# Front pairs of a two-layer hybrid encoder: products P2 and P4 summed in PSUM, the second pair on sums that stay on chip, norms turned later

## The chip, the cores and the metric

One core of one Trainium2 chip runs the whole program in one launch. The metric is the time of an execution on the device in microseconds (us). An engine works through its own instruction list in order; engines wait for each other through semaphores. The names are those of the profile: PE is TensorE (matmuls), PEld its weight loads, DVE VectorE, ACT ScalarE, POOL GpSimd, SP SyncE, which here only issues transfers.

## The reference

All 512 tokens go through two layers of the same form, 2048 features wide.

```python
def hybrid_layer(x, w_in, w_out, g_pre, g_post, w_alpha, b_alpha, g_gla, g_att, rel_bias):
    h = rmsnorm(x, g_pre)
    z = h @ w_in
    gq, gk, gv, gg, ga, aq, ak, av, ag = split_columns(z)
    log_a = jax.nn.log_sigmoid((ga @ w_alpha + b_alpha).astype(jnp.float32)) / GLA_TAU
    o_gla = gla_chunk_causal(gq, gk, gv, log_a)          # reshapes to heads left out
    o_gla = rmsnorm(o_gla, g_gla) * jax.nn.silu(gg)
    o_att = chunk_band_attention(aq, ak, av, rel_bias)
    o_att = rmsnorm(o_att, g_att) * jax.nn.silu(ag)
    y = jnp.concatenate([o_gla, o_att], axis=-1) @ w_out
    return x + rmsnorm(y, g_post)
```

The change concerns the columns `ag` and `gg` of the input projection (the two gates, each two blocks of 512 columns) and the silu behind them.

## The kernel before, in words

**Products.** A pair of 512-column blocks of the input projection is computed with seven products in place of eight, by a fast scheme for 2 x 2 blocks. The activations are cut into two token halves and two feature halves (A11, A12, A21, A22), the weights into blocks of the pair. P1 and P2 use A11 and A12, P4 uses A22, and P5, P6, P3, P7 use the sums S1, S2, S4, S3 of these blocks. Each product has four contraction chunks `c` of 256 rows. Operands are kept as a high and a low part, so one chunk is 12 matmuls of 128 x 512: two halves of the chunk, two token tiles `t`, three combinations (high x high, high x low, low x high). "A product" below is one such chunk.

**What a product needs.** `Job.load` fetches its weight tile on SP's queue (512 KB; `raw`, or `H` for the tile that lives through a pair). `Job.high` casts it to its high part `wh` on ACT, after DVE has added `raw` to `H` (P5, P6, P4) or subtracted (P7). `Job.low` makes the low part `wl` on DVE. Four buffers each of `raw`, `H`, `wh` and `sa`, three of `wl`, and `ahead()` keep this some three to five products ahead of TensorE.

**Results.** A `Pair` accumulates in PSUM in two banks X, two banks Y and, for early pairs, two banks Z. `copies` keeps a result in SBUF (`ev`) by ACT; `combine` adds a kept copy to a finished bank by DVE into a temporary `t`, and `gate_consume` puts the silu (ACT, L781) on it and stores it by POOL.

**Front.** Each layer starts with two early pairs, `FRONT` = (AG0, AG1), (GG0, GG1). First come P1 and P2 of pair 0 and of pair 1 (the head), then P5, the middle (P6 and P3 mixed), P7 and P4 of pair 0, and the same of pair 1. Then the AV pair and the rest of the layer follow. Beside the products run tasks, advanced by `pump`, so many steps per product (`rate`): `token_sums` makes the 16 sums (DVE L683; split by ACT L109 and DVE L110; stored to DRAM by POOL), from `full` tiles such as `g8` and `g11`. Pair 0 (`direct`) takes the sums from SBUF and reads only A22 back (`sa<-A`); pair 1 reads all 16 sums (`sa<-S`) and A22 again, 512 KB each, on SP's queue.

**Norms.** `token_norms` squares the token rows (ACT L506), takes the power -1/2 on POOL (L493), turns the result with a TensorE transpose (L586) and stores the row. In layer 0, `first_norms(1)` and `load_forget_gate(0)` (which loads w_alpha and casts it, L763) stand in the task list ahead of the head. The order in which tasks and products issue instructions in the program is the order on each engine.

Of the kernel before, what the change touches and what calls it, by code (L numbers as in the profile page):

```python
# [35 lines left out]
def hybrid_trunk(  # L36
# [113 lines left out]
    PROD_END = early_head(C_END) + early_rest(C_END)  # L150
    LEFT = {"P5": "S1", "P6": "S2", "P3": "S4", "P7": "S3", "P4": "A22"}
# [6 lines left out]
    class Job:  # L158
# [8 lines left out]
        def load(self):  # L167
# [29 lines left out]
            src = (so_d if end else sa_d)[self.l].get((LEFT.get(k), c))  # L197
# [38 lines left out]
    for l in range(L):  # L236
        infos = [{"early": True, "direct": True}, {"early": True, "second": True}]
        for (b0, b1), pr in zip(FRONT, infos):
            stream += [Job(l, k, c, b0, b1, pr) for k, c in early_head(C_IN)]
# [130 lines left out]
    class Pair:  # L370
        def __init__(self, l, pair, consume, feature_major=False, early=False, end=False, scaled=True, direct=False,
                     y_banks=pair_banks):
            self.l, self.b0, self.consume = l, pair[0], consume
            self.feature_major, self.early, self.end = feature_major, early, end
            self.scaled, self.direct = scaled, direct
            self.banks = {"X": pair_banks, "Y": y_banks, "Z": aux_banks}
            self.target = {"P1": "X", "P5": "Y", "P6": "X", "P3": "Y", "P7": "X", "P2": "Y", "P4": "X"}
            self.starts = ["P1", "P5", "P2"]
            if early:
                self.target.update(P2="Z", P4="Y")  # L380
                self.starts.append("P4")
# [3 lines left out]
        def copies(self, name, src):  # L385
            self.keep[name] = []
            for t in range(2):
# [5 lines left out]
                self.keep[name].append(e)  # L393

# [11 lines left out]
        def finished(self, k, t):  # L406
# [12 lines left out]
        def operand(self, job, k, c):  # L419
            if job.a is not None:  # L420
                return job.a
            if k in ("P1", "P2", "P4"):
# [6 lines left out]
        def matmuls(self, job, k, c):  # L429
# [5 lines left out]
            for kk in range(2):  # L435
                if self.feature_major:
# [11 lines left out]
                else:  # L448
                    for t in range(2):
                        tok = slice(kk * 256 + t * P, kk * 256 + (t + 1) * P)  # L450
                        ops = ((0, job.wh), (0, job.wl), (1, job.wh))
                        for m, (part, rhs) in enumerate(ops):
                            nc.tensor.matmul(  # L453
                                out_ps[t], a[:, part, tok], rhs[:, kk, :],
                                start=(fresh and kk == 0 and m == 0),
                                stop=(c == self.last and kk == 1 and m == 2), skip_group_check=True,
                            )
            spent.add((self.l, LEFT.get(k), c))

        def run(self, prods, rate=0.0, skip=0, after=None):  # L460
            pace = Pace(rate, skip)
            for k, c in prods:
# [3 lines left out]
                if c == self.last:  # L466
# [48 lines left out]
    def load_row(half, j, src, q):  # L515
# [3 lines left out]
        elif j == 0:  # L519
            row = [slot(tag, [1024]) for tag in XS1]  # L520
# [29 lines left out]
    def load_first(i):  # L550
# [7 lines left out]
        if i in (5, 7, 12, 14):  # L558
            half, j = divmod((5, 7, 12, 14).index(i), 2)
            with tc.issue_after(last_load[0]):  # L560
                rows[half, j] = load_row(half, j, x, nc.sync)
# [13 lines left out]
    def token_norms(l, half, xs):  # L575
# [9 lines left out]
        ps = aux()  # L585
        nc.tensor.transpose(ps[0:2, 0:P], r, ident)  # L586
        row = t2((P,))
        nc.vector.tensor_copy(row[0:2], ps[0:2, 0:P])
        nc.gpsimd.dma_start(r_d[l][half], row[0:2])
        normed.add((l, half))  # L590
        yield
# [123 lines left out]
    def token_sums(l):  # L715
        order = products(C_IN, "S1") + [({"P6": "S2", "P3": "S4"}[k], c) for k, c in middle(C_IN)]
        order += products(C_IN, "S3")
        return make_sums(
            l, False, STAGE,
            lambda c: (full[0, c][:, 0, :], full[0, c][:, 1, :], full[1, c][:, 0, :], full[1, c][:, 1, :]), order=order,  # L720
# [50 lines left out]
    tasks.append(first_norms(1))  # L771
    tasks.append(load_forget_gate(0))

    def layer(l):
# [102 lines left out]
        if l:  # L877
# [3 lines left out]
            Pair(l, FRONT[0], gate_consume(1), early=True, scaled=False, direct=True, y_banks=aux_banks),  # L881
            Pair(l, FRONT[1], gate_consume(0), early=True, scaled=False),
# [6 lines left out]
        front[1].run(early_rest(C_IN), rate=0.25)  # L889
        drain()  # L890
# [571 lines left out]
```

## Time and profile before

| | |
|---|---|
| median of 3 runs (lowest to highest) | 1642.57 us (1642.13 to 1644.08) |
| profiled execution | 1638.18 us, span 1636.4 us |
| granted TensorE clock, mean | 0.995 |
| busy: PE, PEld, DVE, ACT, POOL | 98%, 83%, 78%, 56%, 10% |
| read from and written to DRAM | 412.93 MB, 71.06 MB; 296 GB/s over the span |
| front of layer 0, of layer 1 (about) | 5 to 198 us, 820 to 1009 us |

PE's busy share counts each matmul up to a modelled end, so that neighbours overlap; where PE is slowed a little, its busy share hardly shows it. The number of matmuls in a stretch does.

### The profile page before, as it was taken

Reading aid. Unit: us, or ns where it says so; the run is one execution under the profiler, and the core shown is the slowest. Engines: PE = TensorE matmul, PEld = TensorE weight load, DVE = VectorE, ACT = ScalarE, POOL = GpSimd, SP = SyncE. Lnnn points to the kernel's source line nnn. Section 1 sums busy time; section 2 is a strip of 40 time slices with the busy share of each in tenths; the row PEclk is TensorE's granted clock in tenths of the full one; section 3 lists DMA queues with packets and bytes.
Section 4 is the critical chain, followed back from the end, with each engine's and each line's share of the span. In section 5 each row is a group of like instructions: output and inputs, shape, how many; then the busy total and the mean of one; then the engine's idle time right before and its main releaser. Section 6 shows DMA issues by size and latency. Waiting matters only on the chain.

```text
span 1636.4 us, 24588 instructions
## 1 busy us (share of the span) xinstructions
PE 1598.3 (98%) x8818; PEld 1354.3 (83%) x8818; DVE 1270.3 (78%) x1626; ACT 918.3 (56%) x1520; POOL 165.8 (10%) x258
## 2 busy tenths in 40 slices
PE   9899999999999999999998999999999999999997
PEld 5577789999988887788786877899999888777886
DVE  7797777786877876778779977777868778766887
ACT  8554544466676545555685545444566765345553
POOL 1120000000101101310122100000011011023100
PEclk9999999999999999999999999999999999999999
DMA  9899987867868698898868998868588686979986
GB/s 370 343 347 372 375 291 249 295 221 248 294 225 292 224 328 307 297 375 313 329 234 303 356 361 342 318 223 314 179 294 291 218 290 216 353 260 349 368 303 235
DMA packets 155419, 486.73 MB, mean 297 GB/s; under 512 B 16956, under 2 KB 36036, under 8 KB 155296
## 3 DMA queue, kind: packets, MB, share of 16 engines
q1 hardware_dynamic: 132704, 406.83, 70.3%
q0 software_dynamic: 22016, 77.37, 12.3%
q8 instruction: 70, 1.15, 0.3%
q10 hardware_dynamic: 576, 0.95, 0.2%
q14 instruction: 53, 0.43, 0.1%
HBM read 412.93 MB, written 71.06 MB: 296 GB/s over the span
## 4 chain that ended last, share of the span: by engine, by line
PE 88%; DMA 5%; DVE 3%; ACT 2%; issue 1%; SPq 0%; DVEq 0%; POOL 0%; POOLq 0%; ACTq 0%
PE mm L453 44%; PE mm L443 20%; PE mm L347 10%; PE ax L453 6%; PE ax L974 2%; DMA raw<-in_w_dram 2%; DMA H<-in_w_dram 2%; DVE wl L227 1%; PE ax L957 1%; PE ax L1140 1%; DMA sa<-A 1%; PE ax L1174 1%; DVE H L211 1%; PE ax L936 1%; PE ax L937 1%
## 5 line engine op out<-in xcount | busy, mean ns | idle before, releaser
L453 PE MATMUL mm<-wh,sa 128*128 128x512 f32 x1536 | 486.3, 392 | 4.5 <-DMA sa<-A 2.1
L222 ACT CAST wh<-H 128x1024 fp32r<-128x1024 f32 x247 | 259.0, 1052 | 244.7 <-PE mm L453 92.7
L222 ACT CAST wh<-raw 128x1024 fp32r<-128x1024 f32 x248 | 261.2, 1053 | 233.7 <-PE mm L453 99.8
L227 DVE TENSOR_TENSOR wl<-H,wh 128x1024 fp32r<-128x1024 f32 (+1 forms) x249 | 302.6, 1218 | 107.0 <-PE mm L453 40.3
L227 DVE TENSOR_TENSOR wl<-raw,wh 128x1024 fp32r<-128x1024 f32 x248 | 303.0, 1223 | 105.2 <-PE mm L453 31.2
L453 PEld LDWEIGHTS mm<-wh,sa 128*128 128x128 f32 x1536 | 287.3, 188 | 68.6 <-issue 3.1
L453 PE MATMUL mm<-wl,sa 128*128 128x512 f32 x768 | 299.8, 390 | 0.0
L443 PE MATMUL mm<-sa,wh 128*128 128x256 f32 x1280 | 237.4, 286 | 0.0
L443 PEld LDWEIGHTS mm<-sa,wh 128*128 128x128 f32 x1280 | 199.8, 191 | 0.3
L453 PE MATMUL mm<-wh,a 128*128 128x512 f32 x576 | 189.4, 397 | 5.1 <-ACT wh L222 3.5
L211 DVE TENSOR_TENSOR H<-H,raw 128x1024 f32<-128x1024 f32 x152 | 184.6, 1220 | 10.3 <-DMA raw<-in_w_dram 6.6
L443 PE MATMUL mm<-sa,wl 128*128 128x256 f32 x640 | 180.6, 283 | 0.0
L453 PEld LDWEIGHTS mm<-wl,sa 128*128 128x128 f32 x768 | 144.2, 188 | 29.4
L453 PEld LDWEIGHTS mm<-wh,a 128*128 128x128 f32 x576 | 106.9, 188 | 34.3 <-ACT wh L222 5.7
L493 POOL TENSOR_TENSOR sm<-sm,mhalf 128x4 f32<-128x4 f32 (+2 forms) x40 | 56.5, 1412 | 756.4 <-DVE sm L990 520.4
L443 PEld LDWEIGHTS mm<-sa,wl 128*128 128x128 f32 x640 | 122.3, 191 | 0.1
L453 PE MATMUL mm<-wl,a 128*128 128x512 f32 x288 | 112.6, 393 | 1.6 <-DVE wl L227 1.6
L443 PE MATMUL mm<-a,wh 128*128 128x256 f32 x512 | 94.9, 285 | 0.0
L347 PE MATMUL mm<-wh,a 128*128 128x512 f32 x256 | 82.8, 393 | 0.0
L443 PEld LDWEIGHTS mm<-a,wh 128*128 128x128 f32 x512 | 80.3, 191 | 0.2
L214 DVE TENSOR_TENSOR raw<-H,raw 128x1024 f32<-128x1024 f32 x64 | 78.2, 1221 | 2.1 <-DMA raw<-in_w_dram 1.6
L443 PE MATMUL mm<-a,wl 128*128 128x256 f32 x256 | 72.4, 283 | 0.0
(206 smaller groups left out, 2358.9 us busy)
## 6 DMA issues: line engine op xcount, KB each, us to landing
raw<-in_w_dram SPq DMA_DIRECT2D x336, 512.0 KB, 5.6
sa<-S SPq DMA_DIRECT2D x192, 512.0 KB, 4.7
H<-in_w_dram SPq DMA_DIRECT2D x63, 512.0 KB, 5.0
sa<-A SPq DMA_DIRECT2D x56, 512.0 KB, 7.4
S<-g POOLq DMA_DIRECT2D x32, 512.0 KB, 4.7
oS<-g POOLq DMA_DIRECT2D x32, 512.0 KB, 6.3
sa<-oS SPq DMA_DIRECT2D x32, 512.0 KB, 5.1
sg<-t POOLq DMA_DIRECT2D x32, 256.0 KB, 5.9
```

Of the source, the lines that this page charges most:

```text
L211: nc.vector.tensor_tensor(out=h, in0=h, in1=r, op=ALU.add)
L214: nc.vector.tensor_tensor(out=r, in0=h, in1=r, op=ALU.subtract)
L222: last_cast[0] = nc.scalar.copy(self.wh, src).ins
L227: last_low[0] = nc.vector.tensor_tensor(out=self.wl[:, kk, :], in0=self.src[:, kk, :], in1=self.wh[:, kk, :].bitcast(F32), op=ALU.subtract ...
L347: mm = nc.tensor.matmul(pss[o], a[:, part, t], rhs[:, kk, :], start=(i == 0 and kk == 0 and m == 0), stop=(i == n - 1 and kk == 1 and m == 2),
L443: nc.tensor.matmul(dst, lhs[:, kk, f], a[:, part, tok], start=(fresh and kk == 0 and m == 0 and ft % 2 == 0), stop=(c == self.last and kk ...
L453: nc.tensor.matmul(out_ps[t], a[:, part, tok], rhs[:, kk, :], start=(fresh and kk == 0 and m == 0), stop=(c == self.last and kk == 1 and m ...
L493: return nc.gpsimd.tensor_tensor(out=out_r, in0=v, in1=mhalf[:, : v.shape[-1]], op=ALU.pow).ins
L936: nc.tensor.matmul(ps[:, :n], self.qh[:, t], self.kl[:, :n], start=False, stop=False)
L937: nc.tensor.matmul(ps[:, :n], self.ql[:, t], self.kh[:, :n], start=False, stop=True)
L957: nc.tensor.transpose(ps[:, j * P : (j + 1) * P], self.prob[i][:, j * P : (j + 1) * P], ident)
L974: nc.tensor.matmul(o, self.pt[i][:, j * P : (j + 1) * P], av[hd // 4, j // 2][:, j % 2, (hd % 4) * P : (hd % 4 + 1) * P], start=(j == 0), ...
```

## The change: seeded PSUM, resident sums, a new head order, later norms

- The head's order becomes P1 of pair 0, P1 of pair 1, P2 of pair 0, P2 of pair 1, at 2.7 task steps per product in place of 2.0.
- A front pair is `seeded`. P2 accumulates into P1's banks X, and the silu reads PSUM directly, without DVE's combine. For P6, `open` takes new banks X and Y, and ACT copies P1's kept result into X. After P7, ACT copies X into Y, and P4 accumulates on Y. The banks Z and the copies of x after P7 are not used any more.
- Pair 1 uses the last eight sums (`SUMS[8:]`) from SBUF, and A22 is loaded once, for both pairs, into slots of `full` tiles (g8, g14, g11, g15).
- The norm's transpose and the store of its row are delayed by eight task steps (`turn`). In layer 0, `first_norms(1)` and `load_forget_gate(0)` go to the front of the task list after the head; the token rows for the second half are loaded at jobs 15 and 17 of the stream (12 and 14 before), into g12 and g13.

```diff
+    SUMS = products(C_IN, "S1") + [({"P6": "S2", "P3": "S4"}[k], c) for k, c in middle(C_IN)] + products(C_IN, "S3")
+    RESIDENT = SUMS[8:] + products(C_IN, "A22")
...
-            if src is not None and (k == "P4" or not (p and p.get("direct"))):
-                until(lambda: (self.l, end, LEFT[k], c) in made)
+            if src is None or p.get("direct") and k != "P4" or p.get("second") and (name, c) in RESIDENT:
+                return
+            until(lambda: (self.l, end, name, c) in made)
+            if p.get("direct"):
+                until(lambda: (self.l, end, "S3", c // 2) in made)
+                self.a = S_on[self.l, name, c] = slot(("g8", "g14", "g11", "g15")[c], [2, 512], F32R)
+            else:
                 self.a = rtile("sa", (2, 512), F32R)
-                nc.sync.dma_start(flat(self.a), src)
+            nc.sync.dma_start(flat(self.a), src)
...
+            if seeded:
+                self.target.update(P2="X", P4="Y")
+                self.starts.remove("P2")
...
+        def open(self, *names):
+            for name in names:
+                self.acc[name] = self.banks[name]()
+            for t in range(2):
+                nc.scalar.copy(self.acc["X"][t], self.keep["p1"][t])
...
+            elif self.seeded:
+                self.consume(0, {"P2": 0, "P4": 1}[k], t, out, None)
...
+                order = [(kk, t) for kk in range(2) for t in range(2)]
+                if self.seeded and (k, c) in (("P7", self.last), ("P4", self.first)):
+                    order.sort(key=lambda z: z[1])
...
+                        if k == "P7" and self.seeded:
+                            for t in range(2):
+                                nc.scalar.copy(self.acc["Y"][t], self.acc["X"][t])
                         for t in range(2):
                             self.finished(k, t)
-                        if k == "P7" and self.early:
+                        if k == "P7" and self.early and not self.seeded:
                             self.copies("x", self.acc["X"])
...
-        if i in (5, 7, 12, 14):
-            half, j = divmod((5, 7, 12, 14).index(i), 2)
+        if i in (5, 7, 15, 17):
+            half, j = divmod((5, 7, 15, 17).index(i), 2)
...
+        def turn():
+            ps = aux()
+            nc.tensor.transpose(ps[0:2, 0:P], r, ident)
...
         normed.add((l, half))
+        delayed.append([8, turn])
...
     tasks.append(prep_first())
-    tasks.append(first_norms(1))
-    tasks.append(load_forget_gate(0))
...
-        for pair in front:
-            pair.run(early_head(C_IN), rate=2.0)
+        for k in ("P1", "P2"):
+            for pair in front:
+                pair.run(products(C_IN, k), rate=2.7)
+        if l == 0:
+            tasks[0:0] = [first_norms(1), load_forget_gate(0)]
+        front[0].open("Y", "X")
         front[0].run(early_rest(C_IN), rate=1.0)
         drain()
         tasks.append(forget_gate())
+        front[1].open("X", "Y")
         front[1].run(early_rest(C_IN), rate=0.25)
```

Three places in the order of instructions. First TensorE in layer 0, before, where P2 of pair 1 starts: `mm_561` and `mm_562` are the banks of pair 1's P1, `ax_704` one of its banks for P2, `a_37` the operand A12, `norm` the norm.

```order
L453 MATMUL mm_561<-wl_575,a_36_329 128x512
L453 MATMUL mm_562<-wh_527,a_36_329 128x512
L453 MATMUL mm_562<-wl_575,a_36_329 128x512
L586 MATMUL ax_671<-cst,norm_208 2x128
L453 MATMUL ax_704<-wh_577,a_37_334 128x512
L453 MATMUL ax_704<-wl_609,a_37_334 128x512
L453 MATMUL ax_705<-wh_577,a_37_334 128x512
```

TensorE after the change, where P5's third chunk starts (`mm_787`, `mm_788` are pair 0's Y banks, `g_89` and `g_93` the sums S1 of the second and third chunk):

```order
L475 MATMUL mm_788<-wl_755,g_89_599 128x512
L475 MATMUL mm_788<-wh_739,g_89_599 128x512
L613 MATMUL ax_1051<-cst,norm_208 2x128
L475 MATMUL mm_787<-wh_758,g_93_622 128x512
L475 MATMUL mm_788<-wh_758,g_93_622 128x512
```

The transpose of the second norm has moved from ahead of P2 of pair 1 to the middle of P5, eight products later.

ScalarE in layer 0 around the start of P5, before. `t_139` is the combined P2 of a pair, `wh_721` and the next two are P5's first casts, the squares of the token rows (L506) stand earlier, among P2's casts:

```order
L506 ACTIVATE t_109_647,sm_639<-sg_618 128x512
L222 CAST wh_694<-raw_666 128x1024
L222 CAST wh_721<-H_211 128x1024
L109 CAST g_127_726<-g_48_388 128x512
L222 CAST wh_745<-H_217 128x1024
L109 CAST g_131_750<-g_61_428 128x512
L222 CAST wh_769<-H_221 128x1024
L109 CAST g_135_774<-g_70_464 128x512
L781 ACTIVATE t_140_799<-t_139_797,norm_208 128x512
```

The same place after. L806 is the silu on pair 1's P2 (`mm_418`, `mm_419`), L531 the squares, L230 the casts of P5, L403 the kept copies of P5, L790 the cast of w_alpha, and the last row P6's first cast:

```order
L806 ACTIVATE t_126_784<-mm_419,norm_208 128x512
L531 ACTIVATE t_135_813,sm_811<-g_97_644 128x1024
L531 ACTIVATE t_136_815,sm_811<-g_98_645 128x1024
L230 CAST wh_712<-H_211 128x1024
L230 CAST wh_739<-H_217 128x1024
L531 ACTIVATE t_141_838,sm_836<-bias_716 128x512
L531 ACTIVATE t_144_844,sm_836<-sg_719 128x512
L230 CAST wh_758<-H_221 128x1024
L230 CAST wh_777<-H_225 128x1024
L403 COPY ev_887<-mm_788 128x512
L790 CAST g_153_890<-g_152_889 98x512
L230 CAST wh_808<-H_211 128x1024
```

The silus of P2 and the squares now stand ahead of P5's first casts, and the kept copies of P5 and the cast of w_alpha ahead of P6's.

SP's queue in layer 0 at pair 1's P6 to P7, before: `sa<-S` are sums, `raw` weights.

```order
L201 DMA sa_1388<-S_90 128x1024
L164 DMA raw_1496<-in_w_dram 128x1024
L201 DMA sa_1417<-S_91 128x1024
L201 DMA sa_1436<-S_98 128x1024
L201 DMA sa_1454<-S_99 128x1024
L164 DMA raw_1517<-in_w_dram 128x1024
L201 DMA sa_1474<-S_92 128x1024
L164 DMA raw_1542<-in_w_dram 128x1024
```

SP's queue after, in layer 0, at pair 0's P5. The loads of A22 into g8 and g11, then a sum for pair 1, w_alpha and the weights of the middle:

```order
L209 DMA sa_1186<-S_84 128x1024
L166 DMA raw_760<-in_w_dram 128x1024
L209 DMA g_186_1080<-A_100 128x1024
L209 DMA g_200_1142<-A_102 128x1024
L209 DMA sa_1221<-S_85 128x1024
L786 DMA g_152_889<-in_w_alpha_dram 98x512
L166 DMA raw_779<-in_w_dram 128x1024
L166 DMA raw_834<-in_w_dram 128x1024
```

The loads of the last eight sums are gone from pair 1; A22's load has moved up, ahead of the weights of pair 0's middle.

More of the change, by code (lines that the diff above doesn't have):

```diff
@@ L421, in operand @@
                 return job.a
-            if k in ("P1", "P2", "P4"):
+            if k in ("P1", "P2", "P4") and (self.l, LEFT.get(k), c) not in S_on:
                 key = {"P1": (0, 0, c), "P2": (1, 0, c), "P4": (1, 1, c)}[k]
@@ L434, in matmuls @@
             fresh = k in self.starts and c == self.first
-            for kk in range(2):
-                if self.feature_major:
+            if self.feature_major:
+                for kk in range(2):
                     for ft in range(4):
@@ L447, in matmuls @@
                             )
[L448 to L457, printed above, removed]
+            if not self.feature_major:
+                order = [(kk, t) for kk in range(2) for t in range(2)]
+                if self.seeded and (k, c) in (("P7", self.last), ("P4", self.first)):
+                    order.sort(key=lambda z: z[1])
+                for kk, t in order:
+                    tok = slice(kk * 256 + t * P, kk * 256 + (t + 1) * P)
+                    ops = ((0, job.wh), (0, job.wl), (1, job.wh))
+                    for m, (part, rhs) in enumerate(ops):
+                        nc.tensor.matmul(
+                            out_ps[t], a[:, part, tok], rhs[:, kk, :],
+                            start=(fresh and kk == 0 and m == 0),
+                            stop=(c == self.last and kk == 1 and m == 2), skip_group_check=True,
+                        )
             spent.add((self.l, LEFT.get(k), c))
@@ L513, in hybrid_trunk, with load_row @@
     XS1 = ("g9", "g10")
-    def load_row(half, j, src, q):
+    def load_row(half, j, src, q, spare=XS1):
         t = 2 * half + j
@@ L519, in load_row @@
         elif j == 0:
-            row = [slot(tag, [1024]) for tag in XS1]
+            row = [slot(tag, [1024]) for tag in spare]
         else:
@@ L557, in load_first @@
             load_gate_columns(0)
-        if i in (5, 7, 12, 14):
-            half, j = divmod((5, 7, 12, 14).index(i), 2)
+        if i in (5, 7, 15, 17):
+            half, j = divmod((5, 7, 15, 17).index(i), 2)
             with tc.issue_after(last_load[0]):
-                rows[half, j] = load_row(half, j, x, nc.sync)
+                rows[half, j] = load_row(half, j, x, nc.sync, XS0[1])
     norm = [small.tile([P, 3, NT], F32, tag="norm", name=nm("norm"), bufs=2) for _ in range(L)]
@@ L584, in token_norms @@
         nc.vector.tensor_tensor(out=norm[l][:, 2, cols], in0=ss, in1=r, op=ALU.mult)
[L585 to L589, printed above, removed]
+        def turn():
+            ps = aux()
+            nc.tensor.transpose(ps[0:2, 0:P], r, ident)
+            row = t2((P,))
+            nc.vector.tensor_copy(row[0:2], ps[0:2, 0:P])
+            nc.gpsimd.dma_start(r_d[l][half], row[0:2])
         normed.add((l, half))
+        delayed.append([8, turn])
         yield
@@ L715, in token_sums @@
     def token_sums(l):
-        order = products(C_IN, "S1") + [({"P6": "S2", "P3": "S4"}[k], c) for k, c in middle(C_IN)]
-        order += products(C_IN, "S3")
         return make_sums(
             l, False, STAGE,
-            lambda c: (full[0, c][:, 0, :], full[0, c][:, 1, :], full[1, c][:, 0, :], full[1, c][:, 1, :]), order=order,
+            lambda c: (full[0, c][:, 0, :], full[0, c][:, 1, :], full[1, c][:, 0, :], full[1, c][:, 1, :]), order=SUMS,
         )
@@ L880, in layer @@
         front = [
[L881 to L885 removed]
+            Pair(l, FRONT[0], gate_consume(1), early=True, scaled=False, seeded=True),
+            Pair(l, FRONT[1], gate_consume(0), early=True, scaled=False, seeded=True),
+        ]
+        for k in ("P1", "P2"):
+            for pair in front:
[3 more added lines that the diff above has]
+        front[0].open("Y", "X")
         front[0].run(early_rest(C_IN), rate=1.0)
@@ L888, in layer @@
         tasks.append(forget_gate())
+        front[1].open("X", "Y")
         front[1].run(early_rest(C_IN), rate=0.25)
+        S_on.clear()
+        for job in stream[: cursor[0]]:
+            job.a = None
         drain()
```

16 lines of the change are left out of this document (8 added, 8 removed).

## The prediction

> **What bounds the kernel now.** The profiled execution took 1638.18 us (span 1636.4), 4.4 us under the median of the three runs, 1642.57. The sum below is made against the 1638.18, and its result is carried to the median as a difference. I read the shares of the chain first.
>
> ```profile
> PE 88%; DMA 5%; DVE 3%; ACT 2%; issue 1%; SPq 0%; DVEq 0%; POOL 0%; POOLq 0%; ACTq 0%
> ```
>
> TensorE sets the end, so only the 12% in which it waits can be won: the change neither adds nor removes a product. The change sits in the front (two column pairs) of each layer, so I cut the front into stretches and counted the product matmuls (L453) in each. The columns are length, TensorE busy (count), weight loads, granted clock, DMA share, GB/s.
>
> ```profile
> 5.00:69.00 64.00, 49.45 (x192) 36.54 (x193) 0.95 1.02 396
> 69.00:87.00 18.00, 16.00 (x64) 11.30 (x63) 1.00 0.65 237
> 87.00:131.00 44.00, 43.20 (x191) 35.27 (x189) 1.00 1.00 371
> 131.00:201.00 70.00, 65.50 (x278) 51.67 (x279) 1.00 0.99 380
> 876.50:896.30 19.80, 14.09 (x51) 10.36 (x51) 0.92 0.74 279
> 896.30:939.43 43.13, 43.13 (x191) 35.69 (x190) 1.00 0.92 344
> 939.43:1011.00 71.57, 66.48 (x286) 52.88 (x285) 1.00 1.00 379
> ```
>
> Busy time flatters, since ends of matmuls overlap; counts don't. The undisturbed pitch comes from the chain's row at 198.17, quoted next: 67.85 / 298 = 0.228 us. A stretch's loss is its length less 0.228 times its count: 3.4 us in 69 to 87 (P5 and the first of P6), 0.5 in 87 to 131 (the rest of pair 0), 6.6 in 131 to 201 (pair 1 and the start of AV); in layer 1, 8.2 in 876.5 to 896.3, nothing in 896.3 to 939.4, and 6.4 in 939.4 to 1011. The head, 5 to 69, also holds start-up and the gate's matmuls, so its own part is read below. Now who is waited for, from the chain of waits (start, length, what):
>
> ```profile
> 167.79 9.01 DMA raw<-in_w_dram
> 176.87 12.44 DMA H<-in_w_dram
> 198.17 67.85 PE mm L453 x298
> 939.43 9.49 DMA sa<-S
> 976.55 6.83 DMA sa<-A
> 983.44 10.12 DMA sa<-A
> ```
>
> Pair 1 waits for transfers in both layers. Stretches of 10 us, all engines (TensorE, its weight loads, VectorE, ScalarE, GpSimd, clock, DMA share, GB/s), show how far that goes and where it stops:
>
> ```profile
> 50.00:60.00 10.00, 4.05 (x11) 3.08 (x11) 4.31 (x7) 6.07 (x13) 1.28 (x2) 0.66 1.03 405
> 80.00:90.00 10.00, 9.04 (x36) 6.52 (x36) 10.00 (x14) 6.67 (x10) 2.67 (x5) 1.00 0.63 222
> 190.00:200.00 10.00, 8.95 (x39) 6.77 (x38) 6.76 (x8) 7.07 (x8) 1.08 (x2) 1.00 1.02 409
> 200.00:210.00 10.00, 10.00 (x46) 8.29 (x45) 10.00 (x10) 5.47 (x7) 0.00 (x0) 1.00 0.56 188
> 890.00:900.00 10.00, 7.87 (x27) 6.30 (x28) 10.00 (x13) 5.24 (x9) 3.20 (x6) 0.83 0.65 223
> 1000.00:1010.00 10.00, 8.60 (x38) 6.48 (x37) 5.72 (x6) 5.54 (x6) 1.10 (x2) 1.00 1.02 406
> ```
>
> Three limits are in these rows. At 190 and 1000 the DMA engines are full at 406 to 409 GB/s, and TensorE makes 38 or 39 matmuls of a possible 44. At 80 and 890 VectorE is full, while DMA has room. At 50 it is a wait of another kind, shown below. From 200 on TensorE is full and DMA half idle: nothing there takes back what the front gains.
>
> **The change, part by part.** Prices of one, first (group rows of the first 1040 us: busy, mean ns, idle before):
>
> ```profile
> L222 ACT CAST wh<-H 128x1024 fp32r<-128x1024 f32 x163 | 170.8, 1052 | 170.8 <-PE mm L453 58.2 <-DVE H L211 57.1 <-PE mm L443 23.6
> L227 DVE TENSOR_TENSOR wl<-H,wh 128x1024 fp32r<-128x1024 f32 x163 | 198.6, 1222 | 72.3 <-PE mm L453 28.9 <-ACT wh L222 19.1 <-PE mm L443 12.3
> L211 DVE TENSOR_TENSOR H<-H,raw 128x1024 f32<-128x1024 f32 x108 | 131.2, 1220 | 9.0 <-DMA raw<-in_w_dram 5.7 <-DMA H<-in_w_dram 2.5
> L392 ACT COPY ev<-mm 128x512 f32<-128x512 f32 x48 | 27.9, 582 | 17.8 <-PE mm L453 11.5 <-PE mm L443 6.2
> L781 ACT ACTIVATE t<-t,norm 128x512 f32<-128x512 f32 x32 | 23.0, 722 | 14.5 <-DVE t L401 12.5 <-DVE t L403 1.3 <-ACT ev L392 0.6
> L506 ACT ACTIVATE t<-g 128x1024 bf16<-128x1024 f32 x12 | 12.6, 1062 | 2.7 <-DMA g<-in_x_dram 2.7
> L506 ACT ACTIVATE t<-bias 128x512 bf16<-128x512 f32 x4 | 2.5, 637 | 0.0
> L506 ACT ACTIVATION_READ_ACCUMULATOR t<-g 128x1 f32 x12 | 2.4, 202 | 0.0
> L401 DVE TENSOR_TENSOR t<-ax,ev 128x512 f32<-128x512 f32 x18 | 12.2, 685 | 0.0
> ```
>
> *Loads (12 fewer per layer).* Pair 1 keeps eight sums and takes A22 from pair 0's load.
>
> ```profile
> sa<-S SPq DMA_DIRECT2D x192, 512.0 KB, 4.7
> sa<-A SPq DMA_DIRECT2D x56, 512.0 KB, 7.4
> ```
>
> At 409 GB/s 512 KB take 1.28 us, so 15.4 us of traffic leave a 70 us stretch whose DMA share is 0.99: about 0.78 remains. The transfer waits should then go; I leave 1.6 us in layer 0 and 1.4 in layer 1 for the casts and the start of AV. Terms: **-5.0** in each layer, bounds 0 (the weights alone still bind: the chain also names raw and H) and -6.6 or -6.4. A22 now waits on SP's queue for the last sums that read g8 and g11, with P6's weights and w_alpha behind it.
>
> *Norms and the head, layer 0.* This is the wait at 50:
>
> ```profile
> 56.15 0.37 PE L586 MATMUL ax<-cst,norm 128*2 128x128 f32 x1 [5.95 <-POOL norm L493]
> 57.17 1.05 PE L453 MATMUL ax<-wh,a 128*128 128x512 f32 x2
> 58.45 1.05 PE L453 MATMUL ax<-wh,a 128*128 128x512 f32 x2
> 892.13 0.50 PE L453 MATMUL ax<-wl,g 128*128 128x512 f32 x1 [2.94 <-DVE wl L227]
> ```
>
> One transpose of the norm stands in TensorE's order and holds P2 of pair 1 for 5.95 us. Then three matmuls take 58.45 - 57.17 = 1.28 us, 0.43 each: the clock is low (0.66 in the row of 50). The row of 50 to 60 has ten matmuls and this transpose, all after 56.15: 3.85 us for what takes 10 x 0.228 = 2.28, so the low clock costs 1.6 us. The change takes both away: term **-7.5**, bounds -7.5 and -3 (if ScalarE's casts then hold the products at 3.3 us instead of 2.7).
>
> But the norm's work is moved, not removed. ScalarE's order now has at the turn from P2 to P5: two silus, two squares of 1024, P5's first cast, its second, four squares of 512, the third. P5 needs its bank empty (the silus) and that cast: 2 x 0.72 + 2 x (1.06 + 0.20) + 1.05 = 5.0 us after P2's end, and the low part on VectorE another 1.22, of which two matmuls hide 0.46: 5.8 in all. The four squares (4 x 0.84) delay the third cast by about as much as two products last, cover that may be just short: 0.2. A wait of this length is followed by the low clock: 1.6. Less 0.6, since the sums that bound VectorE in 69 to 87 are drawn earlier. Term **+7.0**, bounds 0 (the squares run before P2 ends) and +8.
>
> *Forget gate, layer 0.* Its weights are now cast on ScalarE between P5's kept copies and P6's first cast. After P5's end: 2 x 0.58 (kept copies), about 0.6 (cast of 512, by the copy), about 0.7 on VectorE (by L401), the adds of H 1.22 each, of which one is needed first, 1.05 for the cast, 1.22 for the low part less 0.46: 5.5, and 1.6 of low clock. From this 3.4 goes, the loss of that place before, and about 1 of silu and combine work that stood there: term **+2.7**, bounds -3.4 and +4.
>
> *Seeding.* Per pair four DVE combines of 0.69 go, and ScalarE gets two more copies on balance (2 x 0.58). A copy by ScalarE into PSUM has no row; the nearest is its copy out of PSUM, 0.58, bounds 0.4 and 1.05. Those after P7 run for one token half while TensorE works on the other (six matmuls, 1.37 us): no cost, at most about 1 us each if a cast of 1.05 stands in front. The seeds of P1 run during P2 or P7. What has a cost is the banks: P5 of pair 1 now uses the bank that P4 of pair 0 has just filled and its two silus must empty, and in layer 1 the same at P2 to P5. One silu and what overlaps: about 1.0 (0.72 and the wake-up). Terms **+1.2** in layer 0 and **+2.0** in layer 1 for two places, bounds 0 and 2.5 each.
>
> *VectorE, layer 1.* In 876.5 to 896.3 it is full. Four combines (2.7 us) leave it ahead of P5, and with 2.7 pump steps per product instead of 2.0 more sums are made in the head. But the rel-bias memsets also stand in its order there and can hold it. Half of the 8.2: term **-4.0**, bounds -8 and +2.
>
> Sum: -5.0 - 5.0 - 7.5 + 7.0 + 2.7 + 1.2 + 2.0 - 4.0 = **-8.6**. I take -9: 1629 for an execution like the profiled one, 1633.5 against the median.
>
> **The clock rule.** By the granted clock and the pitch, a wait of 5.95 was followed by a low clock, and one of 2.94 as well (0.83 in the row of 890). The Trainium skill, "TensorE: Matmul & The Clock Gate", Part 1, says that the array falls to half speed after an idle window of about 3.4 us and needs about as long of work to come back. The row of 2.94 is below that figure, so the trace decides (shorter waits before it may share the window); if the page's window held here and the two new waits of layer 0 stayed under it, 3.2 would leave the sum, which would be -12.
>
> **Rivals.**
> *Everything hides.* The squares and the forget gate's cast find ScalarE idle before P2 and P5 end, so the wait of 5.95 goes and nothing takes its place. Then -7.5 - 3.4 - 6.6 - 8.2 - 6.4 = -32, and with the bank waits (3.2) and one wait of some 2 us left, -27: 1615.5. For it: ScalarE is busy only 6.07 of 10 us at 50. Against: its order is fixed, and the silus ahead of the squares wait for TensorE.
> *The weights bind anyway.* The two chain rows of layer 0 name raw and H, not the sums. If their rings, not the traffic, time them, the -10 fails: +1.4, 1644. Against: 1.02 of DMA share at 190 and 1000.
> *Slower: SP's queue.* w_alpha's load stands behind two A22 loads, which wait for sums, and two raw tiles of the middle stand behind it. If w_alpha lands after P5's end (it is free to start only when the squares of g12 are done, some 4 us into the wait of P5, and P5 lasts 11), ScalarE holds P6 for what is left. A late A22 (7.4 to land), then a late raw (5.6): +13 on -8.6, so about +4, 1647. It decides the sign from some 9 us of delay on. Against: P5's eleven us cover one landing.
>
> **How the numbers follow.** A measurement can tell this kernel from itself to about 0.2%, 3.3 us. Chances: the forecast, -4 to -18, 0.52; everything hides, -18 to -28, 0.20; the weights bind or terms cancel, within 3.3, 0.13; SP's queue or the new waits longer than priced, 0.15. So faster 0.72, same 0.13, slower 0.15. The likeliest time is 1633.5, its own range 1625 to 1638.5. For 8 in 10 I take 1617 to 1646, which leaves out the ends of the first and last rival.
>
> **What would show it.** Right: TensorE's wait for the norm gone, and in its place a wait for a cast of wh at the turn from P2 to P5 in layer 0 and another before P6; the DMA share of pair 1 under 0.85 with 43 or more matmuls per 10 us; no silu waiting for L401. Wrong: a DMA of raw or w_alpha as releaser in layer 0's P6, VectorE held by memsets in layer 1's head, or a pair 1 that still runs at 1.00 of DMA share.

## The result and the profile after

| | before | after |
|---|---|---|
| median of the runs shown with the result (4 each) | 1643.32 us | 1631.65 us |
| ratio, 95% interval | | 0.9931 [0.9908, 0.9954] |
| a second series (22 and 5 runs) | 1642.12 us | 1630.86 us |
| ratio, 95% interval | | 0.9932 [0.9918, 0.9946] |
| profiled execution; span | 1638.18; 1636.4 us | 1635.39; 1633.6 us |
| a second profiled execution; span | 1643.05; 1641.3 us | 1633.26; 1631.5 us |
| read from DRAM | 412.93 MB | 400.35 MB |

The change is 0.7% faster, 11.2 us by the second ratio. Predicted were 9 us, 1633.5 in a range of 1617 to 1646, with a chance of 0.72 for faster. The first pair of profiles shows only 2.8 us between the two kernels, the second pair 9.8: one execution differs from the next by several us, so no single pair of traces gives the gain. The starts of the product matmuls show where executions differ. Between 247 and 766 us the two profiles of each kernel run at a constant distance (1.57 us before, 1.84 after). The differences arise mostly in the fronts, where transfers are full.

One sentence ahead of the prediction is wrong: that the order in which the program issues work is the order on each engine. The traces show otherwise. The memset of the bias tables, written behind the AV pair (which starts at 998 us in layer 1), runs on VectorE during P1 and P2 of layer 1:

```profile
846.79 0.11 DVE L949 MEMSET bias<- 64x64 f32 x1
857.36 0.11 DVE L949 MEMSET bias<- 64x64 f32 x1 [3.86 <-DMA bias<-in_rel_dram]
```

Before, the same two ran at 868.05 and 869.86, though the edit does not name them: an edit moves more than its own lines. The orders quoted there are those of the built programs, so the steps built on them stand. One count beside them is wrong: the transpose of the second norm stands six products later than before (four of P2 and two of P5), not eight.

The stretches of product matmuls after (the boundaries are where the same products start; columns as in the prediction):

```profile
65.30:85.40 20.10, 14.91 (x48) 10.57 (x48) 0.83 1.03 395
...
132.00:201.00 69.00, 68.28 (x298) 55.88 (x299) 1.00 0.86 304
879.90:905.10 25.20, 22.35 (x96) 17.86 (x96) 1.00 1.02 416
905.10:943.00 37.90, 37.08 (x144) 28.56 (x144) 0.91 0.84 303
943.00:1011.00 68.00, 67.64 (x298) 55.86 (x299) 1.00 0.85 299
```

By pitch and count, pair 1 and the start of AV now lose 69.0 - 298 x 0.228 = 1.1 us in layer 0 and nothing in layer 1, where 6.6 and 6.4 were lost before. P5 of layer 0 starts 3.6 us earlier. But it takes 20.1 us for 48 matmuls (10.9 at full pitch). In stretches of 10 us, first one of before, then after:

```profile
70.00:80.00 10.00, 8.95 (x37) 6.26 (x35) 10.00 (x14) 6.75 (x10) 2.14 (x4) 1.00 0.76 266
```

```profile
60.00:70.00 10.00, 5.91 (x17) 3.97 (x16) 6.26 (x9) 7.88 (x16) 2.61 (x6) 0.76 1.03 419
70.00:80.00 10.00, 9.47 (x37) 7.11 (x36) 4.75 (x7) 2.10 (x2) 1.81 (x2) 0.90 1.03 377
80.00:90.00 10.00, 5.70 (x17) 3.81 (x16) 7.63 (x9) 5.58 (x7) 0.00 (x0) 0.83 0.80 301
190.00:200.00 10.00, 10.00 (x46) 8.29 (x45) 9.09 (x8) 6.44 (x7) 0.38 (x1) 1.00 0.58 207
1000.00:1010.00 10.00, 10.00 (x46) 8.29 (x45) 9.86 (x10) 8.43 (x10) 1.08 (x2) 1.00 0.70 228
```

At 190 and 1000 the DMA share fell from 1.02 to 0.58 and 0.70, and TensorE is full. Between 70 and 80, where VectorE was full before, it is busy for 4.75 us now and the DMA engines are full instead. TensorE's long waits around it go back to ScalarE all the same. These are its waits at the start of P5 and of P6, and the largest in pair 0 of layer 1:

```profile
65.39 1.22 PE L475 MATMUL mm<-wh,g 128*128 128x512 f32 x2 [3.79 <-ACT wh L230]
66.92 0.79 PE L475 MATMUL mm<-wl,g 128*128 128x512 f32 x1 [0.30 <-DVE wl L235]
85.44 2.17 PE L475 MATMUL mm<-wh,g 128*128 128x512 f32 x4 [4.30 <-ACT wh L230]
905.13 1.22 PE L475 MATMUL mm<-wh,g 128*128 128x512 f32 x2 [2.22 <-ACT wh L230]
```

ScalarE and then VectorE before the two waits of layer 0 show the two chains that the prediction read from the order: silus, squares, cast; kept copies, w_alpha's cast, its subtraction, two adds of H, cast:

```profile
60.97 1.37 ACT L806 ACTIVATE t<-mm,norm 128x512 f32<-128x512 f32 x2 [4.80 <-PE mm L475]
62.23 1.05 ACT L531 ACTIVATE t<-g 128x1024 bf16<-128x1024 f32 x1
63.27 1.04 ACT L531 ACTIVATE t<-g 128x1024 bf16<-128x1024 f32 x1
64.31 1.03 ACT L230 CAST wh<-H 128x1024 fp32r<-128x1024 f32 x1
...
80.47 1.28 ACT L403 COPY ev<-mm 128x512 f32<-128x512 f32 x2 [3.24 <-PE mm L475]
81.65 0.62 ACT L790 CAST g<-g 98x512 fp32r<-98x512 f32 x1
84.34 1.04 ACT L230 CAST wh<-H 128x1024 fp32r<-128x1024 f32 x1 [2.07 <-DVE H L219]
```

```profile
82.31 0.69 DVE L791 TENSOR_TENSOR g<-g,g 33x512 fp32r<-33x512 f32 x1 [3.82 <-ACT g L790]
83.02 2.36 DVE L219 TENSOR_TENSOR H<-H,raw 128x1024 f32<-128x1024 f32 x2
```

In layer 1 the wait at 905.13 is one for weights, through VectorE's add:

```profile
902.70 1.23 DVE L219 TENSOR_TENSOR H<-H,raw 128x1024 f32<-128x1024 f32 x1 [4.95 <-DMA raw<-in_w_dram]
```

SP's queue shows what fills the DMA engines there. These are issues of layer 0, before from 55 to 90 us (first two rows), and after from 58 to 76 us:

```profile
55.57 1.61 SPq L201 DMA_DIRECT2D sa<-A  x2
58.15 28.09 SPq L164 DMA_DIRECT2D raw<-in_w_dram  x6
```

```profile
58.51 2.14 SPq L209 DMA_DIRECT2D g<-A  x2
61.97 0.32 SPq L209 DMA_DIRECT2D sa<-S  x1
63.84 0.40 SPq L786 DMA_DIRECT2D g<-in_w_alpha_dram  x1
65.73 2.82 SPq L166 DMA_DIRECT2D raw<-in_w_dram  x2
71.11 2.38 SPq L948 DMA_DIRECT2D bias<-in_rel_dram  x2
75.63 0.33 SPq L209 DMA_DIRECT2D sa<-S  x1
```

Before, pair 0's A22 tiles sat in the ring `sa` until P4 and so kept pair 1's sums out. With A22 in other slots the ring is empty, and pair 1's first sums are fetched from 54 us on, during P2 and during P5 of pair 0, among its weights (before, the first was issued at 119.35).

Where the time went, from all traces of the two kernels and of two experiments (lengths in us, between the starts of the same product matmul, each product 12 of them in the order of the trace; every stage at full pitch is 10.9 per four products):

```
                              before  again   after  again | resident  reload
layer 0  P1, P1, P2 (12)       50.95  52.99   43.79  45.08 |   51.90   43.90
         P2 of pair 1 (4)      12.85  13.11   16.08  16.08 |   13.28   16.08
         P5, middle (12)       36.54  36.57   43.71  43.02 |   35.37   45.06
         P7, P4 (8)            21.76  21.76   22.90  23.51 |   23.42   24.79
         pair 1's rest (20)    60.62  60.57   55.86  56.92 |   57.66   60.18
         AV to layer 1        634.85 634.58  636.10 635.43 |  634.30  634.71
layer 1  P1, P2 (16)           53.51  53.52   55.98  55.84 |   54.26   55.17
         P5, middle (12)       41.18  41.26   39.51  35.71 |   40.23   33.04
         P7, P4 (8)            21.76  21.76   23.61  24.24 |   22.84   23.01
         pair 1's rest (20)    59.48  62.45   55.01  55.04 |   54.94   58.70
         AV to the end        637.66 637.71  635.54  635.53 |  635.52  635.62
```

### The profile page after: what moved, and what is told of

It is laid out like the page before. It is cut to its first block, busy times and chain, and to the rows that moved or that the text cites. A ratio compares the mean times of both kernels' runs of the same rounds, so it can differ in the third digit from the quotient of the medians.

```text
span 1633.6 us, 24495 instructions
## 1 busy us (share of the span) xinstructions
PE 1603.0 (98%) x8818; PEld 1359.0 (83%) x8818; DVE 1261.9 (77%) x1610; ACT 921.7 (56%) x1528; POOL 163.9 (10%) x258
## 3 DMA queue, kind: packets, MB, share of 16 engines
HBM read 400.35 MB, written 71.06 MB: 289 GB/s over the span
## 4 chain that ended last, share of the span: by engine, by line
PE 88%; DMA 4%; DVE 4%; ACT 2%; issue 1%; SPq 0%; DVEq 0%; POOLq 0%; ACTq 0%
PE mm L475 48%; PE mm L462 20%; PE mm L356 10%; DMA raw<-in_w_dram 3%; PE ax L1007 2%; DVE wl L235 1%; PE ax L475 1%; PE ax L990 1%; PE ax L1173 1%; PE ax L1207 1%; DMA H<-in_w_dram 1%; ACT wh L230 1%; DVE H L219 1%; PE ax L969 1%; PE ax L970 1%
## 5 line engine op out<-in xcount | busy, mean ns | idle before, releaser
L475 PE MATMUL mm<-wh,sa 128*128 128x512 f32 x1344 | 425.3, 391 | 0.2
L230 ACT CAST wh<-H 128x1024 fp32r<-128x1024 f32 x247 | 259.5, 1052 | 237.1 <-PE mm L475 102.9
L230 ACT CAST wh<-raw 128x1024 fp32r<-128x1024 f32 x248 | 261.2, 1053 | 225.7 <-PE mm L475 108.9
L475 PEld LDWEIGHTS mm<-wh,sa 128*128 128x128 f32 x1344 | 251.3, 188 | 54.0 <-issue 1.5
L475 PE MATMUL mm<-wl,sa 128*128 128x512 f32 x672 | 262.6, 391 | 0.4 <-DVE wl L235 0.4
L475 PE MATMUL mm<-wh,a 128*128 128x512 f32 x704 | 228.6, 395 | 2.6 <-ACT a L109 1.7
L475 PE MATMUL mm<-wh,g 128*128 128x512 f32 x576 | 185.4, 402 | 12.0 <-ACT wh L230 10.3
L475 PEld LDWEIGHTS mm<-wh,a 128*128 128x128 f32 x704 | 131.7, 188 | 35.3 <-issue 4.1
L475 PEld LDWEIGHTS mm<-wl,sa 128*128 128x128 f32 x672 | 126.2, 188 | 26.7 <-DVE wl L235 0.8
L475 PEld LDWEIGHTS mm<-wh,g 128*128 128x128 f32 x576 | 110.9, 194 | 38.7 <-ACT wh L230 12.5
L475 PE MATMUL mm<-wl,a 128*128 128x512 f32 x352 | 138.0, 394 | 0.0
L475 PE MATMUL mm<-wl,g 128*128 128x512 f32 x288 | 114.8, 401 | 2.0 <-DVE wl L235 2.0
L356 PE MATMUL mm<-wh,a 128*128 128x512 f32 x256 | 82.9, 393 | 0.0
```

The source lines that it names most:

```text
L230: last_cast[0] = nc.scalar.copy(self.wh, src).ins
L356: mm = nc.tensor.matmul(pss[o], a[:, part, t], rhs[:, kk, :], start=(i == 0 and kk == 0 and m == 0), stop=(i == n - 1 and kk == 1 and m == 2),
L475: nc.tensor.matmul(out_ps[t], a[:, part, tok], rhs[:, kk, :], start=(fresh and kk == 0 and m == 0), stop=(c == self.last and kk == 1 and m ...
```

## The experiments

All were timed beside the kernel before. "Gain" is (1 - ratio) x 1642 us, with the interval of the ratio.

| run | median us | ratio [95%] | gain us |
|---|---|---|---|
| the change again | 1630.86 | 0.9932 [0.9918, 0.9946] | 11.2 |
| resident_only: before + resident sums | 1632.62 | 0.9952 [0.9939, 0.9966] | 7.9 |
| reload: the change - resident sums | 1638.85 | 0.9981 [0.9968, 0.9994] | 3.1 |
| squares_late | 1630.57 | 0.9920 [0.9900, 0.9941] | 13.1 |
| gate_late | 1628.31 | 0.9918 [0.9898, 0.9938] | 13.5 |
| sum_loads_in_order | 1643.26 | 1.0003 [0.9991, 1.0015] | -0.5 |
| front_order | 1634.90 | 0.9953 [0.9938, 0.9967] | 7.7 |
| front_order_squares | 1633.55 | 0.9940 [0.9926, 0.9953] | 9.9 |
| unseeded | 1630.83 | 0.9925 [0.9907, 0.9944] | 12.3 |
| unseeded_squares | 1628.62 | 0.9929 [0.9917, 0.9942] | 11.7 |
| turn_at_once | 1633.91 | 0.9957 [0.9943, 0.9970] | 7.1 |

**The two kernels again.** For the change:

> The changed kernel once more, for a second profile and a closer time. The first profiles differ by 2.8 us (1635.39 against 1638.18) while the timed runs differ by 11.7. Theory A (a marginal idle stretch at the start of layer 1 trips the low clock in some executions): the time spreads over 1629 to 1636, and a profile of a faster execution has no low clock at 817 to 823 us and its front of layer 1 starts some 3 us earlier. Theory B (the spread lies in the transfers): the start of layer 1 is the same in both profiles, and a stretch with a full DMA share differs.

For the kernel before:

> The kernel before once more, for a second profile. Theory A: stretches without idle time near 3 us repeat to 0.1 us, and what differs from the first profile is a low clock in one place. Theory B: the pair 1 stretches, bound by transfers, differ by several us.

Theory B holds for most of the spread: the pair 1 stretch of layer 1 took 59.48 in one profile of before and 62.45 in the other, and the start-up of layer 0 differs by 2 us, while VectorE-bound and matmul-bound stretches repeat to 0.1. Theory A fell: the low clock at the start of layer 1 (last section) is in both profiles of the change.

**Residency alone, and the change without it.** The first adds to the kernel before only `RESIDENT`, the test in `load` and the A22 slots. The second is the change with

```diff
-    RESIDENT = SUMS[8:] + products(C_IN, "A22")
+    RESIDENT = []
...
-            if p.get("direct"):
-                until(lambda: (self.l, end, "S3", c // 2) in made)
-                self.a = S_on[self.l, name, c] = slot(("g8", "g14", "g11", "g15")[c], [2, 512], F32R)
-            else:
-                self.a = rtile("sa", (2, 512), F32R)
+            self.a = rtile("sa", (2, 512), F32R)
```

> The kernel before with one part of the change alone: pair 1 keeps the last eight sums and A22 is loaded once. If the transfers bound pair 1 (the prediction's terms, -5.0 in each layer; in the traces the two pair 1 stretches shrank by 6.7 and 7.4 us): 8 to 14 us faster than before, 1629 to 1635. Rival (the gain of pair 1 comes from the seeding, which takes combines and copies away): within 3 us of before.

> The change without that part: pair 1 reads all 16 sums and A22 again. If residency carries the gain, and the rest (norms, seeding, head order) comes to +1 to +4 by the trace (layer 0 until pair 1: +4.4, layer 1 until pair 1: +2.7, less the wait for the norm already in it): 1641 to 1648, no faster than before. Rival (seeding and norms carry it): 1630 to 1635, as fast as the change.

The gains add up: 7.9 + 3.1 = 11.0, against 11.2 for both. Residency is the larger part, at the lower edge of the 8 to 14 us expected, but the rest is not the loss of 1 to 4 us that I expected of it. The chain of waits from 130 us on shows the cause. With residency alone, pair 1 is one row of matmuls to the AV pair; without it in the change, sums and A22 are waited for as before:

```profile
135.32 69.90 PE mm L461 x307
```

```profile
127.94 12.04 DMA sa<-S
...
178.64 11.18 DMA sa<-A
```

In the residency-only kernel the wait for the norm is still there, as it should be:

```profile
56.94 0.37 PE L594 MATMUL ax<-cst,norm 128*2 128x128 f32 x1 [5.90 <-POOL norm L501]
```

**The squares and w_alpha's cast later.** The tasks enter after two products of P5, and each square is held behind the latest cast:

```diff
-        if l == 0:
-            tasks[0:0] = [first_norms(1), load_forget_gate(0)]
         front[0].open("Y", "X")
-        front[0].run(early_rest(C_IN), rate=1.0)
+        rest = early_rest(C_IN)
+        front[0].run(rest[:2], rate=1.0)
+        if l == 0:
+            tasks[0:0] = [first_norms(1), load_forget_gate(0)]
+        front[0].run(rest[2:], rate=1.0)
```

> The change with the squares of the second token half and the cast of w_alpha issued two products later, behind the casts of P5 and the first of P6. In the two profiles of the change the turn from P2 to P5 in layer 0 loses 7.7 us and the step from P5 to P6 6 to 7. Theory (ScalarE's order there takes back what the norm gave): both shrink to the silus and one cast, about 3 and 2 us, with no low clock: 7 to 11 us faster than the change, 1620 to 1624. Rival (VectorE's adds of H or the late weights bind there anyway): at most 3 us faster, 1628 to 1631.

The gain over the change is about 2 us (13.1 against 11.2, intervals overlap; one of its five executions, 3216.61 us, lies outside all others and is not explained). So the theory was half right. The wait at P2 to P5 fell from 3.79 to 1.71 us, though the low clock that was to go with it still came (0.83 from 60 to 70 us). The wait before P6 fell by 1 us only, and is now for the weights that VectorE adds:

```profile
62.42 0.73 PE L475 MATMUL mm<-wh,g 128*128 128x512 f32 x2 [1.71 <-ACT wh L230]
81.52 1.22 PE L475 MATMUL mm<-wh,g 128*128 128x512 f32 x2 [3.25 <-ACT wh L230]
```

```profile
79.11 1.23 DVE L219 TENSOR_TENSOR H<-H,raw 128x1024 f32<-128x1024 f32 x1 [3.46 <-DMA raw<-in_w_dram]
```

The rival, late weights, was the second limit behind ScalarE's order in this run.

**Only w_alpha's cast later.** `load_forget_gate(0)` becomes a task after pair 0's products, its load behind the latest weight load, its cast behind the latest cast.

> The change with only the cast of w_alpha (and its load) moved, to pair 0's end. Theory: the step from P5 to P6 in layer 0 loses the kept copies, an add and a cast, 3 to 4 us in place of 6 to 7, and the turn from P2 to P5 stays: 2 to 4 us faster than the change, 1627 to 1629. Rival (the adds of H wait for weights that land late): no difference, 1630 to 1632.

Of the stage P2 to the middle, 4 us go, and the wait before P6 is 1.62 us in place of 4.30: that chain was read rightly. But P7 of pair 0 then takes 5 us more than in the change, with a wait of 3.48. It is not the moved cast that holds it: w_alpha is only fetched at 130.4 us in this run. VectorE waits 3.18 us for a late weight tile to add to `H`, and the low part that TensorE needs stands behind that add. So late weights took back what the moved cast gave: pair 1 starts at 133.3 us in this trace, at 132.0 and 132.8 in the change's. Gain over the change: 2 us, within the intervals.

```profile
82.60 0.73 PE L475 MATMUL mm<-wh,g 128*128 128x512 f32 x2 [1.62 <-ACT wh L230]
...
117.29 0.80 PE L475 MATMUL mm<-wl,g 128*128 128x512 f32 x1 [3.48 <-DVE wl L235]
```

```profile
114.88 1.23 DVE L219 TENSOR_TENSOR H<-H,raw 128x1024 f32<-128x1024 f32 x1 [3.18 <-DMA raw<-in_w_dram]
116.02 1.22 DVE L235 TENSOR_TENSOR wl<-raw,wh 128x1024 fp32r<-128x1024 f32 x1
```

**Loads of sums behind their own weights.** First for all pairs, then for the front pairs alone (this is the second edit; the first has no condition):

```diff
-            nc.sync.dma_start(flat(self.a), src)
+            front = p.get("direct") or p.get("second")
+            with tc.issue_after(last_load[0]) if front else nullcontext():
+                nc.sync.dma_start(flat(self.a), src)
```

> The change with every load of a sum or of A22 issued behind the weight load of its own product (before, the buffers of sa held pair 1's loads back; with the change they start during pair 0's P5). In the change's profiles raw tiles for P6 of layer 1 land 15 to 20 us after their issue, against 5.6 in the median. Theory (these early loads delay the weights): layer 1's stretch from the middle to P4 loses its 4 to 5 us: 3 to 6 us faster than the change, 1625 to 1628. Rival (the loads must be moved at some time, and now stand in pair 1): no difference, 1629 to 1632.

> As the last but one test, but the loads are tied to their product's weights in the two front pairs alone, so the later pairs keep the change's order (there the tie cost some 10 us, outside the stretch in question). Theory (early loads of pair 1's sums and of A22 delay the weights of pair 0): in layer 1 P6 to P4 of pair 0 lose nothing, in layer 0 pair 0's middle starts earlier but pair 1 starts about as late as in that test (its front of layer 0 was 5 us longer, that of layer 1 2 to 5 us shorter than the change's): 1628 to 1633. Rival (the early loads are a gain on the whole, since they use idle transfer time): 1634 to 1640.

The first edit was too wide: it also held the loads of the later pairs, which cost 7 us behind layer 1's front alone (642.5 against 635.5 us to the end), so it says little about the front. The second is clean, and the theory fell: 3.5 us slower than the change. In layer 1, P5 to P4 of pair 0 lose less (57.5 us against 63.1 and 60.0), so the early loads do delay the weights there. But what they delay is given back: with the loads in order, P4 of pair 0 and P5 of pair 1 in layer 0 take 33.0 us against 23.4 and 24.6, with forget-gate matmuls and casts waited for there. The chain of waits leads through two weight transfers:

```profile
113.44 14.82 DMA raw<-in_w_dram
...
128.32 11.34 DMA H<-in_w_dram
```

So transfers hold that stretch. Why these two come later than in the change, when its DMA engines are as full there (1.02 and 1.03), isn't settled.

**Both together.**

> Both: the loads of the front in order, and the squares and w_alpha's cast later. If the late weights were what remained at P5 to P6 when the squares were moved (2 us gained of the 7 to 11 expected), both together gain 5 to 9 us on the change: 1622 to 1626. Rival (VectorE's adds of H after P5's low parts bind): no more than the squares alone, 1628 to 1631.

It is 2.2 us better than the ordered loads alone, as the squares alone were better than the change, and not better than the squares alone. So neither range holds: it is slower than the squares alone. P5 of layer 0 takes 16.04 us, but the ordered loads alone had already brought it to 15.95 (squares alone 19.10); what the squares add is the 2 us at P2 to P5. P4 to P5 kept its cost (33.3 us).

**Without seeding.** `seeded=False` for both pairs, no `open`, pair 0's Y in the auxiliary banks as before.

> The change without seeding: P2 goes to banks of its own, VectorE combines, P4 starts fresh, no bank is shared between the pairs; head order, norms and resident sums stay. The prediction's terms for the banks (+1.2 and +2.0) and half of VectorE's (-4.0): within 2 us of the change, 1629 to 1633, with no wait at P4 to P5 and at layer 1's P2 to P5. Rival (VectorE's combines cost more than the banks): 3 to 6 us slower than the change, 1634 to 1637.

Seeding is worth nothing that can be measured (12.3 and 11.2, overlapping). The trace shows both sides. The bank waits of the change are gone, and VectorE, which combines again, holds P5 of layer 1 longer (14.68 us against 11.93 and 12.15), while the middle behind it is shorter (21.76 against 27.58 and 23.55). The bank waits in the change's second profile (the first has only the one at P2 to P5 of layer 1, 0.91):

```profile
132.77 0.49 PE L475 MATMUL mm<-wh,sa 128*128 128x512 f32 x1 [0.72 <-ACT t L806]
...
880.96 0.50 PE L475 MATMUL mm<-wh,g 128*128 128x512 f32 x1 [0.76 <-ACT t L806]
...
940.91 0.50 PE L475 MATMUL mm<-wh,sa 128*128 128x512 f32 x1 [0.73 <-ACT t L806]
```

**No seeding, and squares later.**

> The change without seeding and with the squares and w_alpha's cast behind P6's first casts, the two that cost nothing or gained. Each was 1 to 2 us faster than the change. If their gains are of different places (no shared banks; ScalarE free at P2 to P5): 3 to 6 us faster than the change, 1625 to 1628. Rival (VectorE, which combines again, binds at P5 of layer 0 as soon as ScalarE does not): 1629 to 1631.

The gains don't add: 11.7. P5 of layer 0 takes 20.5 us, with waits of up to 2.55 us for casts. The median, 1628.62, lies between the two ranges, and the gain over the change by the ratios, 0.5 us, is nearer to the rival's; that VectorE is its cause isn't shown.

**The transpose without its delay.** `turn()` in place of `delayed.append([8, turn])`.

> The change without the eight steps of delay: the norm's transpose and row store are issued at once, but the second half's norm stays behind the head. In its order the second transpose stands at the same place, inside P5, and the first at the end of P1 of pair 1. Theory (moving the norm behind the head took the wait of 5.95 us away, the delay is worth nothing): as the change, 1629 to 1633, P2 of pair 0 and pair 1 without a wait for the norm. Rival (the delay does it): a wait for the norm of several us at the first or second transpose, 1633 to 1638.

No wait for the norm returns; its front stages lie within those of the change's two profiles or 1 us beside them, and its span is 1631.8 us. So the delay is not what took the 5.95 us away; the place of the norm behind the head is what remains (the new order of the head was not run without it). The time alone, 1633.91, lies in the rival's range: timed it is 4 us slower than the change by the ratios and 3 by the medians, with intervals that just overlap (0.9943 to 0.9970, 0.9918 to 0.9946). No stretch of its profile accounts for that, and it stays open.

No version here beats the change clearly. The best, gate_late and squares_late, are 2 us faster inside the intervals.

## Why the prediction was right, point by point

The time and the direction were right; some terms only by balance.

- *Loads, -5.0 in each layer.* The mechanism is shown: residency alone gains 7.9 us, and taking it out of the change loses 8.1. In the traces the term itself is larger: by pitch and count the loss fell from 6.6 to 1.1 us in layer 0 and from 6.4 to nothing in layer 1. Some 5 to 8 us of that was spent again in layer 1 before pair 1, which the prediction had only as a rival: the loads that remain moved to where the weights of P5 and P6 are fetched.
- *Norms and head, -7.5.* The last matmul of P2 of pair 1 starts at 61.22 in place of 68.79 us; the first twelve products take 7 to 8 us less. Right: the wait for the norm is gone, and it is there still (5.90) with residency alone. The task's new place is the step that did it as far as is shown.
- *P2 to P5, +7.0.* Measured in the first profile: a wait of 3.79 us and a low clock, together 7.7 us over full pitch from the last product of P2 to the end of P5's third. In the second profile it is 6.2. The cause is right and the size agrees, but partly by balance: the waits were 3.79 and 0.30 us where 6 were worked out, in part because the silu on the first bank already starts at 60.97, ahead of P2's last matmul; and the low clock cost about 3.2 us by the pitch where 1.6 stood. The squares moved away took 2 us of it.
- *Forget gate, P5 to P6, +2.7.* A chain of 4.30 and 0.53 us of waits and a low clock, 7.3 us in all (8.1 in the second profile), where 7.1 were worked out ahead of subtracting what had been lost there. That chain is right by the rows; but the same stretch had lost 3.1 us before, not the 4.4 that were subtracted, so the term came out at about +4 and +5, at and above its bound of +4. With squares and cast moved away 3.25 us of wait stay, for late weights; with the cast and its load alone moved 1.62 stay, and a late weight is waited for at P7.
- *Banks, +1.2 and +2.0.* Waits of 0.72, 0.76 and 0.73 us in the second profile, one in layer 0 and two in layer 1: 2.2 us where 3.2 were predicted; 0.91 in the first. The return of seeding, VectorE's combines, was counted in the next term; without seeding the time is the same within the intervals, so both cancel.
- *VectorE, layer 1, -4.0.* This is the step that failed. P5 and the middle took 1.7 to 5.5 us less, but P7 and P4 took 2.2 more and the head of layer 1 2.4 more (with a bank wait of 0.91 or 0.76 in it), so to the start of pair 1 the layer gained between -2.7 and +0.7 us. The run without residency shows what the term would have been: 111.2 us to that point in place of 116.4, a gain of 5.2, and with the loads in order it is 112.7. So the early loads of pair 1's sums and of A22 took it. The memset that the prediction feared in layer 1's head did hold VectorE (3.86 us), but the only wait of TensorE behind it in the head is the one for a bank.
- *SP's queue as a rival* was the right place with the wrong price: A22 and sums (in layer 0 w_alpha too) stand ahead of the middle's weights, and in layer 1 raw tiles come late (add at 902.70, waiting 4.95 us for one). It cost 4.6 to 7.9 us against the run without residency, in layer 1 rather than layer 0, not 13, and did not turn the sign. In layer 0's P6 no transfer held TensorE until squares and cast were moved.
- *Everything hides* did not happen, for the reason given: the order on ScalarE is fixed behind TensorE.

The predicted DMA share of pair 1, 0.78, was measured as 0.85 to 0.86 over the stretch, so the mark "under 0.85" was just missed, with 46 matmuls per 10 us where 43 were named as the mark. The rule of the Trainium skill, "TensorE: Matmul & The Clock Gate", Part 1, on idle windows of about 3.4 us is taken up in the last section; both new waits of layer 0 were longer than 3.4 us, so page and trace agree on them.

## What to carry to other kernels

Where a stretch is bound by transfers, read what its loads are and leave out those whose data is still on chip; that was worth 0.5% here and adds up with other gains. When a buffer ring is relieved, ask what its fullness was holding back: the loads it delayed now start early and meet others. And a piece of work that is taken out of one wait (the norm ahead of P2) stands at the front of another engine's queue somewhere; look in the built order for the next instruction that has to wait behind it.

## What the runs showed of the hardware

Several short waits close together can bring the low clock, without one long one. At the end of layer 0 (last products, ahead of layer 1) TensorE waits like this in the change:

```profile
812.33 0.73 PE L356 MATMUL mm<-wh,g 128*128 128x512 f32 x2 [0.83 <-ACT wh L230]
813.59 0.50 PE L356 MATMUL mm<-wl,g 128*128 128x512 f32 x1 [0.53 <-DVE wl L235]
817.73 0.27 PE L613 MATMUL ax<-cst,norm 128*2 128x128 f32 x1 [1.58 <-POOL norm L518]
818.27 0.73 PE L356 MATMUL mm<-wh,g 128*128 128x512 f32 x2 [0.27 <-ACT wh L230]
819.53 0.80 PE L356 MATMUL mm<-wl,g 128*128 128x512 f32 x1 [0.53 <-DVE wl L235]
```

The same stretch before and after, and then in squares_late and in front_order (each from about 3 us ahead of the norm's transpose):

```profile
815.00:825.00 10.00, 7.67 (x32) 5.53 (x31) 6.98 (x12) 10.00 (x17) 1.80 (x3) 1.00 0.57 175
```

```profile
815.00:825.00 10.00, 7.63 (x26) 5.42 (x25) 7.34 (x12) 9.71 (x16) 1.80 (x3) 0.83 0.51 167
```

```profile
810.00:820.00 10.00, 7.64 (x26) 5.36 (x25) 7.35 (x12) 9.63 (x16) 1.79 (x3) 0.83 0.51 170
```

```profile
820.00:830.00 10.00, 7.63 (x33) 5.50 (x32) 6.80 (x11) 10.00 (x18) 1.79 (x3) 1.00 0.59 177
```

After the change there are 26 matmuls in place of 32 at a granted clock of 0.83: 1.4 us by the pitch, in both profiles of the change. It would be natural to blame the wait of 0.83, the one that the first profile of before lacks. The other traces speak against it:

| trace | waits of TensorE there, us | sum | granted clock |
|---|---|---|---|
| before | 0.53, 1.54, 0.26, 0.53 | 2.86 | 1.00 |
| the change | 0.83, 0.53, 1.58, 0.27, 0.53 | 3.74 | 0.83 |
| front_order | 0.85, 0.53, 1.58, 0.27, 0.53 | 3.76 | 1.00 |
| squares_late | 1.57, 0.26, 0.52 | 2.35 | 0.83 |

The low clock is in nine of the fourteen traces, and neither the number of waits nor their sum decides which. What does isn't shown. Nor is it all of why AV to layer 1 takes 0.6 to 1.5 us longer after the change: residency alone has the low clock too and takes 634.30 us there, less than before. No single wait there is over 1.6 us. By the Trainium skill, "TensorE: Matmul & The Clock Gate", Part 1, an idle window of about 3.4 us is needed. The runs do not agree with a reading in which one gap must fill the window.
